# Own buffers for single-head ropes, an earlier zero for the sigmoids, early weight units around the norms, and two banks for the sparse transposes in a two-layer hybrid trunk

## The chip, the cores and the metric

The kernel runs on one core of a Trainium2 chip. The metric is the device time of one execution in microseconds. A core has five engines with queues of their own: TensorE (PE, matrix products, with its weight loads listed as PEld), VectorE (DVE), ScalarE (ACT), GpSimd (POOL) and SyncE (SP, which here issues nearly all DMA transfers). Each queue runs in the order in which it was written; semaphores tie the queues together. SBUF is the on-chip memory of 128 partitions, and PSUM the eight banks into which PE writes.

## The reference

Two layers over 256 tokens of width 1024. Each layer makes one wide projection of `x`, runs three token mixers on slices of it, merges them by sigmoid gates, projects, normalises, and follows with a squared-ReLU MLP, a gated per-layer embedding and a second norm. All is float32.

```python
for i in range(DEPTH):                        # 2
    h = x @ w_in[i]                           # 1024 -> 6222 columns
    (fq, fk, fv, ff_logit, sq, sk, sv, dq, dk, dv, iq, ik, iw, g) = split_cols(h)
    o_fox = fox_attention(fq, fk, fv, log_sigmoid(ff_logit + b_forget[i]))   # 6 heads
    o_sb = stick_breaking_attention(sq, sk, sv)                              # 5 heads
    dq, dk, iq, ik = (rope(a, pos) for a in (dq, dk, iq, ik))
    o_dsa = dsa_attention(dq, dk, dv, iq, ik, iw)   # 5 heads, one key head, top 64 keys
    gates = sigmoid(g.reshape(b, s, 3, D_MODEL))
    merged = (gates[:, :, 0] * (o_fox @ w_up_fox[i]) + gates[:, :, 1] * (o_sb @ w_up_sb[i])
              + gates[:, :, 2] * (o_dsa @ w_up_dsa[i]))
    x = layer_norm(ALPHA * x + merged @ w_out[i], ln1_g[i], ln1_b[i])
    ffn = square(relu(x @ w_ff_in[i])) @ w_ff_out[i]        # width 4096
    ple = sigmoid(x @ w_ple_gate[i]) * (p[i] @ w_ple[i])
    x = layer_norm(ALPHA * x + ffn + ple, ln2_g[i], ln2_b[i])
```

## The kernel before

**Precision and weight units.** Each float32 operand is split into a high and a low part of the matmul type fp32r, and a product is three matmuls: high by high, high by low, low by high (`mm3`, L158). Weights are loaded in units of 512 KB or less, mostly 128 partitions by 2 blocks by 512 columns. `wunit` loads a unit into one of five `wr` buffers by SP (L99), ACT copies it to `wh` (L143) and DVE subtracts to get `wl` (L144); `wh` and `wl` have five buffers each. Every other float32 tile of 512 columns comes from the pool `t2k` with 22 buffers, tiles of 256 columns from `t1k`, 384 columns from `t15` with two buffers.

**Products.** `xstat` multiplies token blocks by a weight slice into two PSUM banks, one per tile of 128 tokens (`pg`, four banks); `wstat` does the transposed product into three. With `by_tile` the token tile 0 is finished first: high products unit by unit (`tile_high`, L211), then the low ones (`tile_low`, L216), then an optional step `mid`, then tile 1. The attention works in four other banks, `ps`.

**A layer in order.** The input projection runs product by product in the list `PRODUCTS`: values of fox, fox queries and keys, index queries (`iq1`, `iq2`), sparse queries and key (`dsa`, done by `c4_done`), stick-breaking (`sb`, a `wstat`), its values with the first sparse query (`sv`, done by `c3_done`), gates. Attention jobs from the list `JOBS` are interleaved with it, one step of each job in flight per 550 columns of product. After them come the gate sigmoids, the three up projections (`up_blocks`, L852 and L853 for the shared blocks), `gated` (products with the gates, L835), the output projection `w_out`, the first norm, the embedding gate product, the MLP in eight chunks (`ff_in`, `ff_out`), and the second norm with the next layer's embedding product and first gate product around it.

**Ropes.** `do_rope` multiplies a slice of PSUM by cosine and sine on DVE (L423, L425, L427) into two `t15` tiles, and POOL adds them (L430, or L432 where the result is doubled). `c2_done`, `c4_done` and `c3_done` use it for 1, 3, 4 and 1 heads. Two calls in a row share the two `t15` buffers.

**Sparse transposes.** `dsa_T` transposes the roped key into one `ps` bank (L636), four blocks of queries into a second (L641), the last query head into a third (L646), each followed by a split.

**Sigmoids.** Their bias tile `zero` is computed by DVE from `last[0]`, a column of the last attention head's transposed and split weights, which makes it wait for that split; the comparison always gives 0. This keeps ACT's table for sigmoids from being loaded amid exponentials.

**Norms.** `layer_norm` takes statistics on DVE, the power on POOL (L255) and two passes on DVE (L259, L261); then the tile is transposed by PE (L178) and split. In the output projection tile 0's norm runs while PE multiplies tile 1; tile 1's norm runs while PE does the embedding product and tile 0 of the gate product. `second_x1T` and `second_T` transpose tile 1 as the `mid` step. At the layer's end the last `ff_out` is done tile by tile for the same reason, and all its four weight units stay in use to its end.

**The planner.** Instructions are put into the engines' queues by a planner that goes by program order among those that its own model of times says are ready, so an instruction late in the program can stand earlier in its queue. `keep_in_program_order` pins single instructions.

Of the kernel before, what the change touches and what calls it, by code (L numbers as in the profile page):

```python
# [16 lines left out]
P = 128  # L17
DM = 1024
T = 256
# [33 lines left out]
def hybrid_trunk(ctx, tc, x, p, w_in, b_forget, w_up_fox, w_up_sb, w_up_dsa, w_out,  # L53
# [25 lines left out]

    def t15(dt=F32R):  # L80
        return act.tile([P, 384], dt, tag="t15", name=nm("t15"), bufs=T15)

    def t16k(dt=F32R):

# [114 lines left out]
    def tok(aT, kb, t):  # L199
        return tuple(a[:, kb, t * P:(t + 1) * P] for a in aT)  # L200

    def xstat(aT, w, l, c0, n, done, nkb=KB, nk=2, by_tile=False, mid=None):


        o = [pg(), pg()]
        units = []

        def tile_high(t, u, wt):
            for kk in range(nk):
                for i in range(2):  # L210
                    nc.tensor.matmul(o[t][:, :n], tok(aT, u * nk + kk, t)[0], wt[i][:, kk, :],  # L211
                                     start=u + kk + i == 0, stop=False)

        def tile_low(t):
            for kb in range(nkb):
                nc.tensor.matmul(o[t][:, :n], tok(aT, kb, t)[1], units[kb // nk][0][:, kb % nk, :],  # L216
                                 start=False, stop=kb == nkb - 1)
            done(t, o[t])

        for u in range(nkb // nk):  # L220
            wt = wunit(wrows(w, l, u * nk, nk, c0, n), nk, n)
            units.append(wt)
            if by_tile:
                tile_high(0, u, wt)
                if u == nkb // nk - 1:
                    tile_low(0)
                    if mid:
                        mid()
                    for v, wt in enumerate(units):
                        tile_high(1, v, wt)  # L230
                    tile_low(1)
            else:
                for t in range(2):
                    for kk in range(nk):
                        kb = u * nk + kk
                        mm3(o[t][:, :n], tok(aT, kb, t), tuple(v[:, kk, :] for v in wt),
                            kb == 0, kb == nkb - 1)
# [54 lines left out]
            nc.scalar.copy(pe[j, t], o)  # L292
        return f

    def ple_products(l, pn):

        q = ps()
        for t in range(2):
            for b in range(2):
                nc.tensor.transpose(q[:, b * T + t * P:b * T + (t + 1) * P], pn[:, t, b * P:(b + 1) * P], ident)  # L300
        pT = tuple(t2k().rearrange("p (k t) -> p k t", t=T) for _ in range(2))
        split(q.rearrange("p (k t) -> p k t", t=T), *pT)

        for j in range(2):
            run(xstat(pT, w_ple, l, j * 512, 512, ple_done(j), nkb=2, nk=2))
            yield

    pe = {}
# [101 lines left out]
    bf = cst.tile([P, L, H_FOX], F32, name="bf")  # L410

    for l in range(L):
        if l:
            tc.keep_in_program_order(nc.scalar.preload_act_table_set("natural_log_exp_and_others"))
        vhl = t16k()[:, 0:3584].rearrange("p (i t c) -> p i t c", i=2, t=2)
        vh, vl = vhl[:, 0], vhl[:, 1]

        def do_rope(t, src, nh, dst, dup=1):

            s3 = src.rearrange("p (h d) -> p h d", d=HD)  # L420
            a = t15(F32)[:, :nh * HD].rearrange("p (h d) -> p h d", d=HD)
            b = t15(F32)[:, :nh * HD].rearrange("p (h d) -> p h d", d=HD)
            nc.vector.tensor_mul(a, s3, rope[:, t, None, :].to_broadcast([P, nh, HD]))  # L423
            hf = HD // 2
            nc.vector.tensor_mul(b[:, :, 0:hf], s3[:, :, hf:HD],  # L425
                                 rope[:, 2 + t, None, 0:hf].to_broadcast([P, nh, hf]))
            nc.vector.tensor_mul(b[:, :, hf:HD], s3[:, :, 0:hf],  # L427
                                 rope[:, 2 + t, None, hf:HD].to_broadcast([P, nh, hf]))
            if dup == 1:
                nc.gpsimd.tensor_add(dst.rearrange("p (h d) -> p h d", d=HD), a, b)  # L430
            else:
                nc.gpsimd.tensor_add(dst.rearrange("p (h d) -> p h d", d=HD),  # L432
                                     a.to_broadcast([P, dup, HD]), b.to_broadcast([P, dup, HD]))
# [1 line left out]

        gates = {}

        def gate(c):
            def done(t, o):
                g = t2k(F32)  # L440
                nc.scalar.copy(g, o)
                gates[c, t] = g
            return xstat(xT, w_in, l, O_G + c * 512, 512, done, by_tile=c == 0,
                         mid=second_T if c == 0 else None)

        def second_T():
            for j in range(2):
                to_xT(1, j)

        if l:  # L450
            run(gate(0))
        else:
            for u in range(1, KB // 2):
                wt = wunit(wrows(w_in, 0, 2 * u, 2, O_G, 512), 2, 512)
                if u == 1:
                    for t, o in ple_o:
# [159 lines left out]

        def c4_done(t, o):
            split(o[:, 320:384], vh[:, t, 768:832], vl[:, t, 768:832])
            do_rope(t, o[:, 0:256], 4, rnd[t][:, 64:320])
            do_rope(t, o[:, 256:320], 1, rnk[t][:, 128:256], dup=2)  # L620
            nc.gpsimd.tensor_copy(rnd[t][:, 320:384], rnk[t][:, 128:192])
            for v in (vh, vl):
                nc.gpsimd.tensor_copy(v[:, t, 832:896], v[:, t, 768:832])
# [9 lines left out]
        def dsa_T():  # L633
            q = ps()
            for t in range(2):
                nc.tensor.transpose(q[:, t * P:(t + 1) * P], rnk[t][:, 128:256], ident)  # L636
            split(q[:, 0:256], *dkT)
            q = ps()
            for b in range(2):
                for t in range(2):  # L640
                    nc.tensor.transpose(q[:, b * T + t * P:b * T + (t + 1) * P],  # L641
                                        rnd[t][:, b * P:(b + 1) * P], ident)
            split(q, *dqT, scale=-SCALE)
            q = ps()
            for t in range(2):
                nc.tensor.transpose(q[:, t * P:(t + 1) * P], rnd[t][:, 256:384], ident)  # L646
            split(q[:, 0:256], *dq4, scale=-SCALE)
            yield


# [24 lines left out]
        def softmax_heads(n, heads, mask):  # L675
# [12 lines left out]
            for i, s in enumerate(ss):  # L688
                mn = small(8)
                for t, sl in tiles:  # L690
                    nc.vector.tensor_tensor_reduce(pr[:, i, sl], s[:, sl], mask(t), 1.0, 3e38,
                                                   ALU.add, ALU.min, mn[:, t:t + 1])
                for t, sl in tiles:
                    nc.scalar.activation(pr[:, i, sl], pr[:, i, sl], AF.Exp, bias=mn[:, t:t + 1],
                                         scale=-1.0, accum_out=mn[:, 2 + t:3 + t])
                nc.vector.reciprocal(mn[:, 4:6], mn[:, 2:4])
                for t, sl in tiles:
                    nc.vector.tensor_scalar(pr[:, i, sl], pr[:, i, sl], mn[:, 4 + t:5 + t], None,
                                            op0=ALU.mult)
                yield  # L700
            pT = (t3k(), t3k())
            for i in range(len(heads)):
# [1 line left out]

                transpose_to(q, [pr[:, i, c * P:(c + 1) * P] for c in range(3)])
                split(q[:, 0:384], pT[0][:, i, :], pT[1][:, i, :])
                last[0] = pT[1].bitcast(F32)[:, i, 0:1]
                yield
            values(n, len(heads), pT)
            yield  # L710
# [274 lines left out]
        next(step)  # L985
        merged(1)
        run(step)
        run(xstat(mT, w_out, l, 512, 512, out_done(1), by_tile=True))


        def pgate_done(j):
# [9 lines left out]
            for j in range(2):  # L1001
                to_x1T(1, j)

        run(xstat(x1T, w_ple_gate, l, 0, 512, pgate_done(0), by_tile=True, mid=second_x1T))


        acc = [[pg() for _ in range(2)] for _ in range(2)]
# [43 lines left out]
        prev = None  # L1051
        for c in range(NC):
            hs = ff_in(c)
            if prev is not None:
                ff_out(c - 1, prev)
            else:
# [1 line left out]
            prev = hs  # L1058
        lg2, lb2 = ln_params(ln2_g, ln2_b, l)
        if l < L - 1:  # L1060
            p1 = load_p(l + 1)
        ff_out(NC - 1, prev)


# [3 lines left out]
        for t in range(2):  # L1068
# [7 lines left out]
            if l < L - 1:  # L1076
                layer_norm(t, st, lg2, lb2, None)
                if t == 0:
                    ple = ple_products(l + 1, p1)
                    next(ple)  # L1080
                    for j in range(2):
                        to_xT(0, j)
# [38 lines left out]
```

## Time and profile before

| | |
|---|---|
| median of 3 runs | 873.22 us (873.03 to 873.7) |
| profiled execution | 872.19 us, span 870.5 us |
| PE busy | 852.0 us (98%) |
| DVE busy | 642.2 us (74%) |
| ACT busy | 472.2 us (54%) |
| POOL busy | 70.2 us (8%) |
| read from HBM | 152.30 MB, mean 177 GB/s moved |
| granted PE clock | 0.997 |

The span is the time from the first to the last instruction of the profiled execution; the device time lies 1.7 us over it. A row of the timeline gives start, duration, engine, line, operation, the tiles written and read, shapes, and in brackets the idle time of that engine before it with what ended it. A row of the waits gives who waited for whom, the total in us, the times and the longest. PE's durations overlap, since matmuls are pipelined: a 128x512 product takes 0.39 us from start to end, and the next begins 0.23 us after it.

### The profile page before, as it was taken

How to read it: one execution, taken by the hardware profiler on the slowest of the kernel's cores; microseconds unless marked ns; L12 is line 12 of the kernel's file. 1: busy time of each engine (PE TensorE's matmuls, PEld its weight loads, DVE VectorE, ACT ScalarE, POOL GpSimd, SP SyncE). 2: the span in 40 equal slices, each digit the busy share in tenths (PEclk: the TensorE clock that was granted, in tenths of full speed). 3: DMA queues.
4: the chain of work that ended last, by engine and by line, in shares of the span. 5: the costliest groups of instructions: out<-in, count | busy, mean ns of one | idle time of the engine just before them, and what ended most of it. 6: DMA issues, size and time to landing. Idle time of an engine off the chain costs nothing.

```text
span 870.5 us, 12949 instructions
## 1 busy us (share of the span) xinstructions
PE 852.0 (98%) x4687; PEld 731.7 (84%) x4687; DVE 642.2 (74%) x1135; ACT 472.2 (54%) x749; POOL 70.2 (8%) x136
## 2 busy tenths in 40 slices
PE   8999999999999999999999999999999999999996
PEld 6998978878788888888879988888787888888885
DVE  6579997779867666666776899868887776666666
ACT  5456667676355444444454566677834654444440
POOL 1013010100011000000000221001001010000100
PEclk9999999999999999999999999999999999999998
DMA  8654665534566666666446647556274656666741
GB/s 286 197 148 125 204 190 166 173 126 161 184 217 199 187 193 192 191 217 217 129 137 176 163 129 221 162 165 184 76 248 136 227 191 190 193 192 194 235 128 49
DMA packets 80209, 154.46 MB, mean 177 GB/s; under 512 B 10257, under 2 KB 25745, under 8 KB 80145
## 3 DMA queue, kind: packets, MB, share of 16 engines
q1 hardware_dynamic: 78544, 149.17, 55.7%
q0 software_dynamic: 1600, 4.46, 1.7%
q8 instruction: 37, 0.61, 0.3%
q14 instruction: 28, 0.22, 0.1%
HBM read 152.30 MB, written 1.05 MB: 176 GB/s over the span
## 4 chain that ended last, share of the span: by engine, by line
PE 45%; DVE 3%; issue 1%; ACT 1%; DMA 0%; POOL 0%; POOLq 0%; DVEq 0%
PE pg L158 24%; PE ps L1017 7%; PE ps L1021 4%; PE pg L211 2%; PE pg L216 1%; PE pg L480 1%; PE pg L483 1%; PE pg L482 1%; DVE wl L144 1%; PE ps L165 1%; PE ps L178 1%; PE ps L158 1%; DMA wr<-in_w_in_dram 0%; DVE x L261 0%; ACT wh L143 0%
## 5 line engine op out<-in xcount | busy, mean ns | idle before, releaser
L144 DVE TENSOR_TENSOR wl<-wr,wh 128x1024 fp32r<-128x1024 f32 (+4 forms) x300 | 340.9, 1148 | 169.0 <-ACT wh L143 167.8
L143 ACT CAST wh<-wr 128x1024 fp32r<-128x1024 f32 (+4 forms) x300 | 292.9, 986 | 292.9 <-PE pg L158 109.2
L158 PE MATMUL pg<-wh,t16k 128*128 128x512 f32 (+4 forms) x792 | 231.1, 366 | 0.1
L158 PE MATMUL pg<-wh,t2k 128*128 128x512 f32 x536 | 168.1, 390 | 0.2 <-ACT t2k L143 0.2
L158 PEld LDWEIGHTS pg<-wh,t16k 128*128 128x128 f32 x792 | 144.4, 188 | 20.7 <-DVE t2k L151 0.7
L158 PE MATMUL pg<-wl,t16k 128*128 128x512 f32 (+4 forms) x396 | 143.6, 363 | 0.3 <-DVE wl L144 0.3
L1017 PE MATMUL ps<-t16k,wh 128*128 128x512 f32 x512 | 127.8, 391 | 0.0
L158 PEld LDWEIGHTS pg<-wh,t2k 128*128 128x128 f32 x536 | 100.7, 188 | 21.1 <-ACT t2k L143 0.4
L1017 PEld LDWEIGHTS ps<-t16k,wh 128*128 128x128 f32 x512 | 93.1, 189 | 17.3
L158 PE MATMUL pg<-wl,t2k 128*128 128x512 f32 x268 | 104.4, 390 | 0.0
L158 PEld LDWEIGHTS pg<-wl,t16k 128*128 128x128 f32 x396 | 74.4, 188 | 9.1 <-DVE wl L144 0.7
L1021 PEld LDWEIGHTS ps<-t16k,wl 128*128 128x128 f32 x512 | 69.8, 190 | 5.0
L1021 PE MATMUL ps<-t16k,wl 128*128 128x256 f32 x512 | 71.4, 282 | 0.0
L158 PEld LDWEIGHTS pg<-wl,t2k 128*128 128x128 f32 x268 | 50.4, 188 | 9.9
L480 PE MATMUL pg<-t16k,wh 128*128 128x256 f32 x176 | 50.5, 287 | 2.9 <-DVE t L427 2.9
L483 PE MATMUL pg<-t16k,wl 128*128 128x256 f32 x176 | 49.8, 283 | 0.0
L482 PE MATMUL pg<-t16k,wh 128*128 128x256 f32 x176 | 49.7, 283 | 0.0
L158 PE MATMUL pg<-wh,t1k 128*128 128x512 f32 x112 | 37.9, 396 | 0.0
L480 PEld LDWEIGHTS pg<-t16k,wh 128*128 128x128 f32 x176 | 33.6, 191 | 3.4 <-issue 3.3
L482 PEld LDWEIGHTS pg<-t16k,wh 128*128 128x128 f32 x176 | 33.7, 191 | 0.0
L483 PEld LDWEIGHTS pg<-t16k,wl 128*128 128x128 f32 x176 | 33.7, 191 | 0.0
L211 PE MATMUL pg<-wh,t16k 128*128 128x512 f32 x80 | 31.5, 394 | 0.6 <-ACT t16k L143 0.6
(196 smaller groups left out, 969.8 us busy)
## 6 DMA issues: line engine op xcount, KB each, us to landing
wr<-in_w_ff_in_dram SPq DMA_DIRECT2D x64, 512.0 KB, 4.4
wr<-in_w_ff_out_dram SPq DMA_DIRECT2D x64, 512.0 KB, 4.1
wr<-in_w_in_dram SPq DMA_DIRECT2D x47, 512.0 KB, 4.2
wr<-in_w_in_dram SPq DMA_DIRECT2D x32, 384.0 KB, 3.7
wr<-in_w_out_dram SPq DMA_DIRECT2D x16, 512.0 KB, 4.4
wr<-in_w_ple_gate_dram SPq DMA_DIRECT2D x16, 512.0 KB, 5.0
wr<-in_w_in_dram SPq DMA_DIRECT2D x16, 256.0 KB, 2.9
wr<-in_w_in_dram SPq DMA_DIRECT2D x8, 390.0 KB, 3.3
```

What stands on the lines that cost most here:

```text
L143: a = nc.scalar.copy(hi, src)
L144: b = nc.vector.tensor_sub(lo, src, hi.bitcast(F32))
L158: nc.tensor.matmul(o, l, r, start=start and i == 0, stop=stop and i == 2, skip_group_check=skip)
L165: nc.tensor.matmul(o, a[i == 2], b[i == 1], start=start and i == 0, stop=stop and i == 2)
L178: tr = nc.tensor.transpose(dst[:, i * P:(i + 1) * P], s, ident)
L211: nc.tensor.matmul(o[t][:, :n], tok(aT, u * nk + kk, t)[0], wt[i][:, kk, :], start=u + kk + i == 0, stop=False)
L216: nc.tensor.matmul(o[t][:, :n], tok(aT, kb, t)[1], units[kb // nk][0][:, kb % nk, :], start=False, stop=kb == nkb - 1)
L480: nc.tensor.matmul(oi, hi, rh, start=kb == 0 and i % 2 == 0, stop=False, skip_group_check=True)
L482: nc.tensor.matmul(oi, hi, rl, start=False, stop=False, skip_group_check=True)
L483: nc.tensor.matmul(oi, lo, rh, start=False, stop=kb == KB - 1, skip_group_check=True)
L1017: nc.tensor.matmul(pz[i], wt[0][:, kk, i * P:(i + 1) * P], x1_both[:, 2 * u + kk, :], start=u + kk == 0, stop=False, skip_group_check=True)
L1021: nc.tensor.matmul(pz[i][:, 0:T], wt[1][:, kk, i * P:(i + 1) * P], x1T[0][:, 2 * u + kk, :], start=False, stop=2 * u + kk == KB - 1, skip_ ...
```

## The change

It has five edits.

- `rope_parts`: a rope of one head takes one tile of a new two-buffer tag `t05` instead of two `t15` tiles. In `c4_done` the key's rope stands before the four-head rope.
- `dsa_T`: the last query head's transposes go into the second half of the key's bank; the reads are two on ACT, then two on DVE.
- `last[0]` is set to the softmax reciprocal instead of a column of the split weights.
- `early_unit` loads a weight unit and splits it block by block into four `t2k` tiles instead of `wh` and `wl`. `xstat` takes such units through `early`. One is made for the embedding gate before the last step of the output projection; one each for the next layer's embedding product and first gate in the last MLP chunk, where `p` is now loaded too. `p_T` transposes `p` before the last `ff_out`. `mid` moves from behind `tile_low(0)` into its middle.
- The load of the table for exponentials moves from the start of layer 2 to the third MLP chunk of layer 1.

```diff
+    def rope_parts(nh):
+        if nh == 1:
+            ab = act.tile([P, 2 * HD], F32, tag="t05", name=nm("t05"), bufs=2)
+            return [ab[:, i * HD:(i + 1) * HD].rearrange("p (h d) -> p h d", d=HD) for i in range(2)]
+        return [t15(F32)[:, :nh * HD].rearrange("p (h d) -> p h d", d=HD) for _ in range(2)]
...
+    def early_unit(srcs, nk, n):
+        raw = wload(srcs, nk, n)
+        hi, lo = [t2k() for _ in range(nk)], [t2k() for _ in range(nk)]
+        for kk in range(nk):
+            split(raw[:, kk, :], hi[kk], lo[kk])
+        return hi, lo
...
-        def tile_low(t):
+        def tile_low(t, mid=None):
             for kb in range(nkb):
+                if mid and kb == nkb // 2:
+                    mid()
...
         for u in range(nkb // nk):
-            wt = wunit(wrows(w, l, u * nk, nk, c0, n), nk, n)
+            wt = early[u] if u < len(early) else blocks_of(
+                wunit(wrows(w, l, u * nk, nk, c0, n), nk, n), nk)
...
                 if u == nkb // nk - 1:
-                    tile_low(0)
-                    if mid:
-                        mid()
+                    tile_low(0, mid)
...
     for l in range(L):
-        if l:
-            tc.keep_in_program_order(nc.scalar.preload_act_table_set("natural_log_exp_and_others"))
...
         if l:
-            run(gate(0))
+            run(gate(0, gate_early))
...
             split(o[:, 320:384], vh[:, t, 768:832], vl[:, t, 768:832])
+            do_rope(t, o[:, 256:320], 1, rnk[t][:, 128:256], dup=2)
             do_rope(t, o[:, 0:256], 4, rnd[t][:, 64:320])
-            do_rope(t, o[:, 256:320], 1, rnk[t][:, 128:256], dup=2)
...
-            split(q[:, 0:256], *dkT)
+            for t in range(2):
+                nc.tensor.transpose(q[:, T + t * P:T + (t + 1) * P], rnd[t][:, 256:384], ident)
+            k, q4 = q[:, 0:T], q[:, T:2 * T]
+            nc.scalar.copy(dkT[0], k)
+            nc.scalar.activation(dq4[0], q4, AF.Copy, scale=-SCALE)
+            nc.vector.tensor_sub(dkT[1], k, dkT[0].bitcast(F32))
+            nc.vector.scalar_tensor_tensor(dq4[1], q4, -SCALE, dq4[0].bitcast(F32), op0=ALU.mult,
+                                           op1=ALU.subtract)
...
-            q = ps()
-            for t in range(2):
-                nc.tensor.transpose(q[:, t * P:(t + 1) * P], rnd[t][:, 256:384], ident)
-            split(q[:, 0:256], *dq4, scale=-SCALE)
...
                 nc.vector.reciprocal(mn[:, 4:6], mn[:, 2:4])
+                last[0] = mn[:, 4:5]
...
-                last[0] = pT[1].bitcast(F32)[:, i, 0:1]
...
-        run(xstat(mT, w_out, l, 512, 512, out_done(1), by_tile=True))
+        step = xstat(mT, w_out, l, 512, 512, out_done(1), by_tile=True)
+        for _ in range(3):
+            next(step)
+        pgate_early = [early_unit(wrows(w_ple_gate, l, 0, 2, 0, 512), 2, 512)]
+        run(step)
...
             hs = ff_in(c)
+            if c == 2 and l < L - 1:
+                tc.keep_in_program_order(nc.scalar.preload_act_table_set("natural_log_exp_and_others"))
+            if c == NC - 1 and l < L - 1:
+                p1 = load_p(l + 1)
+                ple_early = [early_unit(wrows(w_ple, l + 1, 0, 2, 0, 512), 2, 512)]
+                gate_early = [early_unit(wrows(w_in, l + 1, 0, 2, O_G, 512), 2, 512)]
...
         if l < L - 1:
-            p1 = load_p(l + 1)
+            pT1 = p_T(p1)
         ff_out(NC - 1, prev)
```

More of the change, by code (lines that the diff above doesn't have):

```diff
@@ L200, in tok, with blocks_of, xstat @@
         return tuple(a[:, kb, t * P:(t + 1) * P] for a in aT)
-    def xstat(aT, w, l, c0, n, done, nkb=KB, nk=2, by_tile=False, mid=None):
+    def early_unit(srcs, nk, n):
[4 more added lines that the diff above has]
+        return hi, lo
+    def blocks_of(wt, nk):
+        return tuple([v[:, kk, :] for kk in range(nk)] for v in wt)
+    def xstat(aT, w, l, c0, n, done, nkb=KB, nk=2, by_tile=False, mid=None, early=()):
         o = [pg(), pg()]
@@ L210, in tile_high @@
                 for i in range(2):
-                    nc.tensor.matmul(o[t][:, :n], tok(aT, u * nk + kk, t)[0], wt[i][:, kk, :],
+                    nc.tensor.matmul(o[t][:, :n], tok(aT, u * nk + kk, t)[0], wt[i][kk],
                                      start=u + kk + i == 0, stop=False)
-        def tile_low(t):
+        def tile_low(t, mid=None):
             for kb in range(nkb):
-                nc.tensor.matmul(o[t][:, :n], tok(aT, kb, t)[1], units[kb // nk][0][:, kb % nk, :],
+                if mid and kb == nkb // 2:
+                    mid()
+                nc.tensor.matmul(o[t][:, :n], tok(aT, kb, t)[1], units[kb // nk][0][kb % nk],
                                  start=False, stop=kb == nkb - 1)
@@ L235, in xstat @@
                         kb = u * nk + kk
-                        mm3(o[t][:, :n], tok(aT, kb, t), tuple(v[:, kk, :] for v in wt),
+                        mm3(o[t][:, :n], tok(aT, kb, t), tuple(v[kk] for v in wt),
                             kb == 0, kb == nkb - 1)
@@ L293, in ple_done, with p_T @@
         return f
-    def ple_products(l, pn):
+    def p_T(pn):
         q = ps()
@@ L302, in ple_products @@
         split(q.rearrange("p (k t) -> p k t", t=T), *pT)
+        return pT
+    def ple_products(l, pT, early=()):
         for j in range(2):
-            run(xstat(pT, w_ple, l, j * 512, 512, ple_done(j), nkb=2, nk=2))
+            run(xstat(pT, w_ple, l, j * 512, 512, ple_done(j), nkb=2, early=early if j == 0 else ()))
             yield
@@ L420, in do_rope @@
             s3 = src.rearrange("p (h d) -> p h d", d=HD)
-            a = t15(F32)[:, :nh * HD].rearrange("p (h d) -> p h d", d=HD)
-            b = t15(F32)[:, :nh * HD].rearrange("p (h d) -> p h d", d=HD)
+            a, b = rope_parts(nh)
             nc.vector.tensor_mul(a, s3, rope[:, t, None, :].to_broadcast([P, nh, HD]))
@@ L436, in hybrid_trunk, with gate @@
         gates = {}
-        def gate(c):
+        def gate(c, early=()):
             def done(t, o):
@@ L443, in gate @@
             return xstat(xT, w_in, l, O_G + c * 512, 512, done, by_tile=c == 0,
-                         mid=second_T if c == 0 else None)
+                         mid=second_T if c == 0 else None, early=early)
         def second_T():
@@ L1002, in second_x1T @@
                 to_x1T(1, j)
-        run(xstat(x1T, w_ple_gate, l, 0, 512, pgate_done(0), by_tile=True, mid=second_x1T))
+        run(xstat(x1T, w_ple_gate, l, 0, 512, pgate_done(0), by_tile=True, mid=second_x1T,
+                  early=pgate_early))
         acc = [[pg() for _ in range(2)] for _ in range(2)]
@@ L1078, in hybrid_trunk @@
                 if t == 0:
-                    ple = ple_products(l + 1, p1)
+                    ple = ple_products(l + 1, pT1, ple_early)
                     next(ple)
```

## The prediction

> **What bounds the kernel now.** I read the engine totals first, then the busy time by stage, then who TensorE (PE) waited for, and last the timeline around each wait.
>
> ```profile
> PE 852.0 (98%) x4687; PEld 731.7 (84%) x4687; DVE 642.2 (74%) x1135; ACT 472.2 (54%) x749; POOL 70.2 (8%) x136
> ```
> ```profile
> core 0: us, PE busy (x) PEld busy (x) DVE busy (x) ACT busy (x) POOL busy (x), PEclk, DMA share, GB/s
> 70.00:113.00 43.00, 41.55 (x316) 38.74 (x315) 40.78 (x116) 26.47 (x54) 9.77 (x20) 1.00 0.60 173
> 113.00:180.00 67.00, 66.67 (x345) 54.60 (x344) 53.43 (x118) 45.65 (x86) 6.52 (x14) 1.00 0.58 174
> 180.00:200.00 20.00, 18.95 (x90) 15.34 (x89) 15.58 (x27) 17.34 (x27) 0.00 (x0) 1.00 0.24 79
> 228.00:245.00 17.00, 16.67 (x79) 13.21 (x79) 13.45 (x19) 8.59 (x13) 2.41 (x2) 1.00 0.50 155
> 433.00:452.00 19.00, 17.79 (x85) 13.61 (x84) 13.64 (x21) 10.10 (x15) 0.99 (x1) 1.00 0.37 105
> 500.00:543.00 43.00, 41.17 (x313) 37.93 (x312) 40.50 (x115) 26.57 (x52) 8.46 (x19) 1.00 0.59 170
> 610.00:630.00 20.00, 18.94 (x92) 15.40 (x91) 15.92 (x25) 17.34 (x27) 0.00 (x0) 1.00 0.23 80
> 657.00:675.00 18.00, 17.68 (x83) 14.06 (x84) 13.46 (x20) 9.74 (x14) 2.39 (x2) 1.00 0.47 146
> 857.00:870.50 13.50, 5.33 (x24) 4.09 (x22) 10.34 (x20) 0.00 (x0) 1.98 (x2) 0.80 0.21 78
> ```
> ```profile
> PE pg L480 <- DVE t L427: 2.9, 2, 1.5
> PE pg L852 <- DVE t2k L835: 2.1, 2, 1.1
> PE ps L178 <- DVE x L261: 0.9, 1, 0.9
> PE ps L646 <- DVE t1k L144: 0.7, 2, 0.3
> ```
>
> PE is the bound: 852.0 of 870.5 us. The change adds no matmul and removes none, so it can only give back idle time of PE. The last stage (8.2 us idle) is the end of the last norm, which the change leaves alone. The eight stages above it hold 1.45 + 0.33 + 1.05 + 0.33 + 1.21 + 1.83 + 1.06 + 0.32 = 7.6 us of idle. That is nearly all there is to win, a little more where a matmul starts late without a gap. The waits name four of the places, each once per layer except L178, which is the change of layer.
>
> **Part A, ropes.** The single-head rope gets buffers of its own, and in `c4_done` the one-head key rope now stands ahead of the four-head query rope.
>
> ```profile
> 78.84 0.73 POOL L430 TENSOR_TENSOR t2k<-t,t 128x256 f32<-128x256 f32 x1 [0.25 <-DVE t L427]
> 78.95 1.30 DVE L144 TENSOR_TENSOR wl<-wr,wh 128x640 fp32r<-128x640 f32 x1
> 80.40 0.18 DVE L427 TENSOR_TENSOR t<-pg,rope 128x32 f32<-128x32 f32 x1
> 80.73 0.36 PE L480 MATMUL pg<-t16k,wh 128*128 128x256 f32 x1 [1.42 <-DVE t L427]
> ```
>
> PE waits at 80.73 for a PSUM bank that the key rope of tile 0 still reads. The key rope could not start before POOL had added the query rope (both `t15` buffers taken), so a weight split of 1.30 us went ahead of it on DVE. With own buffers the key rope is three short instructions (0.1 to 0.2 us each) ahead of the query rope, which ends just before the add at 78.84. The bank is then free near 79.3, where PE's gap begins (80.73 less 1.42): 1.42 us goes, 1.46 us in layer 2 by the same wait (2.9 in the list). But DVE is busy 40.78 of 43 us here, and what it did in PE's gap it must do later. The nearest bound for the gain is from 0 (DVE carries it all on) to 2.9. I take 2.4, near the upper end, because the weight splits run far ahead of PE: counted in order, the one at 78.95 is for the fifth block of a product of which PE is at the first at 80.73. What is late next is the work behind it in the same DVE queue, the top-k and the ropes of the next product.
>
> The two POOL rows that follow bear on what DVE's and POOL's overlap costs.
>
> ```profile
> 109.97 0.32 POOL L430 TENSOR_TENSOR t2k<-t,t 128x64 f32<-128x64 f32 x1
> 110.66 1.22 DVE L144 TENSOR_TENSOR wl<-wr,wh 128x1024 fp32r<-128x1024 f32 x1
> 110.82 1.24 POOL L430 TENSOR_TENSOR t2k<-t,t 128x64 f32<-128x64 f32 x1 [0.24 <-DVE t L427]
> 112.27 0.60 PE L641 MATMUL ps<-ident,t2k 128*128 128x128 f32 x4
> ```
>
> The same add takes 0.32 us alone and 1.24 beside a split, and it ends at 112.06, just ahead of the transposes that need it. So if PE comes here 1.4 us early and DVE does not, up to 1.2 us per layer of part A returns as a wait. [...]
>
> **Part B, sparse transposes.** The last pair of transposes moves into the bank of the first pair.
>
> ```profile
> 113.42 0.42 DVE L144 TENSOR_TENSOR t1k<-ps,t1k 128x256 fp32r<-128x256 f32 x1
> 113.90 0.44 PE L646 MATMUL ps<-ident,t2k 128*128 128x128 f32 x2 [0.33 <-DVE t1k L144]
> ```
>
> PE waited for the first of three banks to be read out; with two banks this wait is gone, 0.33 us each (0.7 in the list). Transposes and reads keep their number and size. Bounds: gain 0.7; or 0, if the second bank waits instead, since ACT now reads two tensors out of the first. I take 0.6.
>
> **Part C, the sigmoids' zero.** The bias that holds the sigmoids back is made from the last softmax reciprocal instead of the last split of the transposed weights.
>
> ```profile
> 179.53 0.17 DVE L696 RECIPROCAL small<-small 128x2 f32<-128x2 f32 x1 [0.74 <-ACT t3k L694]
> 184.79 1.06 ACT L143 CAST wh<-wr 128x1024 fp32r<-128x1024 f32 x1 [1.60 <-issue]
> 187.35 0.54 DVE L144 TENSOR_TENSOR t3k<-ps,t3k 128x384 fp32r<-128x384 f32 x1
> 187.85 1.28 ACT L961 ACT_TABLE_LOAD   x1
> 190.65 0.50 PE L852 MATMUL pg<-wh,t1k 128*128 128x512 f32 x1 [1.05 <-DVE t2k L835]
> 191.92 5.63 ACT L961 ACTIVATE t2k<-t2k,small 128x512 f32<-128x512 f32 x9
> ```
>
> The zero may now come at 179.7 instead of 187.9. All exponentials are over by then, so the table load (1.28 us) and the first sigmoids (0.63 us each, 5.63 over 9) fit in the ACT pauses before 187.85, such as the 1.60 us before 184.79. The gate products then free the banks before PE asks: 1.05 us per layer goes. Bounds: gain 2.1; loss under the first rival. I take 1.9.
>
> **Part D, the norm inside a layer.** One gate-weight unit is split during the output projection into `t2k` tiles, and the transposes of tile 1 move to the middle of tile 0's low products.
>
> ```profile
> 210.23 1.50 SPq L99 DMA_DIRECT2D wr<-in_w_out_dram  x2
> 213.10 0.37 SPq L99 DMA_DIRECT2D wr<-in_w_ple_dram  x1
> 217.00 1.05 ACT L143 CAST wh<-wr 128x1024 fp32r<-128x1024 f32 x1 [1.94 <-DMA wr<-in_w_out_dram]
> 221.43 0.39 PE L211 MATMUL pg<-wl,t16k 128*128 128x512 f32 x1
> 224.13 0.69 DVE L975 SCALAR_TENSOR_TENSOR x<-x,pg 128x512 f32<-128x512 f32 x1 [1.88 <-PE pg L216]
> 240.44 0.50 PE L211 MATMUL pg<-wh,t16k 128*128 128x512 f32 x1 [0.29 <-ACT t16k L143]
> ```
>
> Behind the transposes PE waits for ACT's copy; four low products (0.23 us a start) now cover it. That is the 0.33 and 0.32 us of these stages; DVE is also rid of 1.22 us of split between the norm's steps. The price is on SP's queue: the early load stands ahead of the last unit of the output projection, which ACT already waits for at 217.00. The two issues from 210.23 are the last of that projection; one buffer later is 213.10, some 1.8 us after the second. Cast (1.05 from 217.00) and split (1.22) end near 219.3, 2.1 us before PE's use at 221.43, so nothing is lost. The early subtractions fit in DVE's 1.88 us pause before 224.13. If the load slips further, up to 1 us per layer is lost. Bounds +2.0 and -0.65; I take 0.6.
>
> **Part E, the change of layer.** One unit each of the embedding product and of the first gate, the transposes of `p`, and the table load move from here into the MLP.
>
> ```profile
> 431.53 2.95 ACT L143 CAST wh<-wr 128x1024 fp32r<-128x1024 f32 x3 [7.79 <-PE pg L158]
> 442.44 0.64 PE ps L178 x4
> ```
>
> At 431.53 ACT had waited 7.79 us for a `wh` buffer: the last MLP chunk holds four of the five, the embedding unit the fifth. With that unit and the first gate unit in `t2k`, the second gate unit gets the buffer, so two splits (1.22 each) and the smaller split of `p` leave DVE's way to tile 1's norm, over 2.4 us, against the 0.9 us for which PE waits at 442.44 (L178 in the list). The stage's idle is 1.21, and late starts stand beside it: I take 1.4; bounds 0 and 2. The three extra splits in halves and two loads fall in the MLP, where DVE is busy 16.15 of 22 us (the row below) and the DMA share is 0.50; without that cover each split would cost its 1.2 us. On SP the two loads and that of `p` go ahead of the last eight MLP units; no quoted row shows how late those may be. The `t2k` pool of 22 holds the eleven early tiles (four for each unit, three for `p`) only while nothing else of the chunk is late.
>
> ```profile
> 411.00:433.00 22.00, 22.00 (x101) 18.32 (x101) 16.15 (x24) 8.74 (x13) 1.00 (x1) 1.00 0.50 150
> ```
>
> **Sum.** 2.4 + 0.6 + 1.9 + 0.6 + 1.4 = 6.9 us. The profiled execution took 872.19 us (span 870.5), 1.0 under the median of 873.22; so 865.3 for such an execution and 866.3 for the median.
>
> **The rivals.** First, slower: ACT's order. Once the zero is early, all twelve sigmoids and the table load (9 us) may be put ahead of the casts that the last attention heads and the next weight units wait for. ACT has only 2.7 us of pauses in 180 to 200, so up to 6 us per layer would be late; some 2 us of it is covered by the prefetched units, and 4 us per layer, 8 in all, would turn the 5.0 us of the other parts into a loss of 3: 876. It decides from about 2.5 us per layer. For it: ACT is busy 17.34 of 20 us, and the nine sigmoids ran in one row. Against: the heads' casts come first in the program. [...]
>
> Second, DVE as the bound: in 70 to 113 and 500 to 543 it is 95% busy, and what A and B take out returns as waits behind its splits. Then 1.9 + 0.6 + 1.4 remain, less about 0.7: 870. Against: the splits' lead.
>
> Third, no change: orders shift all over the queues with the planner's times and new waits of a few tenths eat the gain: 873. Fourth, more than forecast: all idle goes and the late starts with it, 7.6 and some 2.1 us (an estimate: about twenty matmuls behind a wait take 0.50, as at 240.44, where the form takes 0.39, as at 221.43): 863.5.
>
> **How the numbers follow.** A difference of 0.2% (1.7 us) is about what a measurement of this kernel can tell from no change. Forecast 0.52, fourth rival 0.10, second 0.18 (all faster): 0.80. No change 0.09, slower 0.11. The forecast's own range is 864 to 869; to hold 8 in 10 it reaches from 863 to 871.5, over the fourth and second, and leaves out the other two (0.20).
>
> **What would show it.** A: no wait of L480 for a rope, the key rope ahead of the query rope. B: no wait at the second bank. C: the table load near 181 and no wait at L852; wrong, if the embedding or up units' casts come after the sigmoids and PE waits for `wl` near 193. D: PE straight from transposes into low products. E: no table load in this stage, tile 1's norm some 2 us sooner, idle in that stage under 0.4 us. The prediction is wrong if the stage from 70 to 113 keeps its 1.4 us of idle under other names.

## The result and the profile after

The changed kernel takes 867.8 us (mean of five executions, 866.8 to 869.6; their median is 867.3) against 873.3 us (mean of six, 872.7 to 873.8; median 873.4) for the kernel before, measured together: a ratio of 0.9937, 95% interval 0.9923 to 0.995, or 5.5 us less. The forecast was 866.3 us, with a range from 863.0 to 871.5. A sixth execution, the profiled one, ran at a granted clock of 0.56 and is left out of these figures, so the trace shown here is that of a repeat of the same kernel (`e1_after` below: median 867.97 us, profiled execution 867.06 us, span 865.3 us).

First the engine totals, then the busy time in the nine stages that the prediction showed (the windows are shifted so that they hold nearly the same work), then the rows of PE's waits that matter here.

```profile
PE 851.3 (98%) x4687; PEld 734.3 (85%) x4687; DVE 640.8 (74%) x1139; ACT 471.8 (55%) x753; POOL 65.8 (8%) x136
```
```profile
core 0: us, PE busy (x) PEld busy (x) DVE busy (x) ACT busy (x) POOL busy (x), PEclk, DMA share, GB/s
70.00:111.80 41.80, 41.58 (x310) 38.95 (x310) 39.45 (x118) 25.69 (x53) 8.06 (x21) 1.00 0.57 169
111.80:178.50 66.70, 66.70 (x358) 55.04 (x357) 54.00 (x116) 45.31 (x83) 7.10 (x15) 1.00 0.60 179
178.50:198.50 20.00, 18.97 (x91) 15.35 (x89) 14.32 (x26) 18.85 (x32) 0.00 (x0) 1.00 0.19 59
226.00:243.00 17.00, 16.96 (x83) 13.78 (x82) 15.72 (x26) 8.55 (x12) 3.29 (x3) 1.00 0.50 163
430.50:449.00 18.50, 18.21 (x89) 15.02 (x88) 13.76 (x21) 7.81 (x12) 1.32 (x2) 1.00 0.31 87
497.20:539.50 42.30, 42.08 (x318) 39.01 (x317) 39.69 (x112) 26.58 (x52) 7.33 (x18) 1.00 0.62 185
605.50:625.50 20.00, 18.82 (x90) 15.22 (x89) 15.44 (x24) 17.31 (x27) 0.00 (x0) 1.00 0.22 67
652.00:670.00 18.00, 17.96 (x87) 14.55 (x87) 15.27 (x22) 9.55 (x14) 3.19 (x3) 1.00 0.37 117
852.00:865.30 13.30, 5.18 (x23) 3.94 (x22) 10.18 (x20) 0.00 (x0) 1.98 (x2) 0.83 0.22 79
```
```profile
PE ps L165 <- ACT t3k L150: 1.6, 2, 0.8
PE pg L165 <- DVE wl L151: 1.1, 3, 0.4
PE pg L500 <- DVE t16k L151: 0.4, 2, 0.2
PE pg L230 <- ACT t16k L150: 0.3, 1, 0.3
```

Read the second fence by window length less PE busy. The rope stages fall from 1.45 and 1.83 us of idle to 0.22 each, the sparse stage after the first from 0.33 to 0.00, the norms inside the layers from 0.33 and 0.32 to 0.04 each, and the change of layer from 1.21 to 0.29. The two stages of the sigmoids do not fall: 1.05 and 1.06 before, 1.03 and 1.18 after. The eight stages together go from 7.6 to 3.0 us of idle.

Idle time is not the whole account: a matmul that starts late without a gap is not in it, and the spans of two traces also differ at the start. PE's 101st matmul is this one (first row before, second row after):

```profile
25.00 0.51 PE L158 MATMUL pg<-wh,t16k 128*128 128x390 f32 x2
26.67 0.51 PE L165 MATMUL pg<-wh,t16k 128*128 128x390 f32 x2
```

Up to it the instructions of every engine and the DMA issues stand in the same order in both kernels, and still the changed kernel is 1.67 us later. In the thirteen traces of this study (the kernel before and the twelve runs below), all with that order, this matmul starts between 25.00 and 27.52 us. So the stages are better compared by how much earlier the same-numbered matmul starts, from one stage to the next; PE has 4687 matmuls in every kernel, and where two kernels do not differ, this count stays within about 0.1 us. Counted so, the change gains 3.7 us in the rope stages and the sparse transposes behind them, loses 0.6 in the sigmoid stages, and gains 1.7 in the norms inside the layers and 2.0 up to and at the change of layer. That is 6.8 us behind the start; less the 1.7 us at the start it gives the 5.2 us by which the span fell.

The list of waits says why the sigmoid stages do not gain. The wait of the up projections for the gate products is gone (2.1 us in the list before). Two others have come: L165 for ACT's copy of attention weights (`t3k`), 1.6 us, and L165 for a weight split (`wl`), 1.1 us where it was 0.3. The timeline shows both:

```profile
180.04 0.15 DVE L981 TENSOR_SCALAR small<-small 128x1 f32<-128x1 f32 x1
181.16 1.28 ACT L984 ACT_TABLE_LOAD   x1
183.81 3.18 ACT L984 ACTIVATE t2k<-t2k,small 128x512 f32<-128x512 f32 x5
187.14 0.48 ACT L150 CAST t3k<-ps 128x384 fp32r<-128x384 f32 x1
187.68 0.49 PE L165 MATMUL ps<-t3k,t16k 128*128 128x512 f32 x1 [0.83 <-ACT t3k L150]
192.68 4.82 ACT L150 CAST wh<-wr 128x1024 fp32r<-128x1024 f32 x5
198.68 0.50 PE L165 MATMUL pg<-wl,t1k 128*128 128x512 f32 x1 [0.38 <-DVE wl L151]
```

The zero is early (180.04) and the table is loaded at 181.16, as forecast. But five sigmoids in a row go ahead of the last head's cast at 187.14, and PE waits 0.83 us for that cast. The weight casts come after all the sigmoids, five in a row from 192.68, and a split is late: DVE makes it from 197.41 on, behind four gate products, and PE has waited 0.38 us when it starts at 198.68. This second wait is gone in `e6_two` and `e9_early_table` below, where ten or all of the sigmoids take the late zero. The transposes that the cast at 187.14 reads were done at 185.92 (three from 185.43, 0.49 us), and the cast ran only after the sigmoids. It is the first rival's mechanism, at 1.2 us per layer in the list.

### The profile page after: what moved, and what is told of

Same layout as the page of the kernel before. It is cut to its first block, busy times and chain, and to the rows that moved or that the text cites. A ratio compares the mean times of both kernels' runs of the same rounds, so it can differ in the third digit from the quotient of the medians.

```text
span 1411.4 us, 12935 instructions
## 1 busy us (share of the span) xinstructions
PE 1401.1 (99%) x4687; PEld 945.7 (67%) x4687; DVE 651.0 (46%) x1139; ACT 476.8 (34%) x753; POOL 61.9 (4%) x136
## 3 DMA queue, kind: packets, MB, share of 16 engines
HBM read 152.30 MB, written 1.05 MB: 109 GB/s over the span
## 4 chain that ended last, share of the span: by engine, by line
PE 98%; issue 1%; DVE 0%; POOL 0%; POOLq 0%
PE pg L165 54%; PE ps L1045 14%; PE ps L1049 7%; PE pg L230 4%; PE pg L500 2%; PE pg L503 2%; PE pg L502 2%; PE ps L172 2%; PE ps L185 2%; PE pg L237 2%; PE ps L165 2%; PE pg L351 1%; PE pg L876 0%; PE pg L875 0%; PE ps L821 0%
## 5 line engine op out<-in xcount | busy, mean ns | idle before, releaser
L165 PE MATMUL pg<-wh,t16k 128*128 128x512 f32 (+4 forms) x792 | 347.8, 527 | 0.0
L165 PE MATMUL pg<-wh,t2k 128*128 128x512 f32 x528 | 257.4, 577 | 0.0
L165 PEld LDWEIGHTS pg<-wh,t16k 128*128 128x128 f32 x792 | 175.7, 225 | 87.5 <-issue 40.9
L1045 PE MATMUL ps<-t16k,wh 128*128 128x512 f32 x512 | 208.8, 575 | 0.0
L165 PE MATMUL pg<-wl,t16k 128*128 128x512 f32 (+4 forms) x396 | 208.6, 527 | 0.0
L165 PEld LDWEIGHTS pg<-wh,t2k 128*128 128x128 f32 x528 | 116.0, 220 | 84.2 <-issue 48.3
L165 PE MATMUL pg<-wl,t2k 128*128 128x512 f32 x264 | 152.0, 576 | 0.0
L1049 PEld LDWEIGHTS ps<-t16k,wl 128*128 128x128 f32 x512 | 103.3, 237 | 22.7 <-issue 12.7
L165 PEld LDWEIGHTS pg<-wl,t16k 128*128 128x128 f32 x396 | 90.6, 229 | 41.6 <-issue 20.3
L1049 PE MATMUL ps<-t16k,wl 128*128 128x256 f32 x512 | 110.6, 385 | 0.0
L165 PEld LDWEIGHTS pg<-wl,t2k 128*128 128x128 f32 x264 | 58.1, 220 | 41.2 <-issue 23.3
L500 PE MATMUL pg<-t16k,wh 128*128 128x256 f32 x176 | 68.5, 389 | 0.0
L502 PE MATMUL pg<-t16k,wh 128*128 128x256 f32 x176 | 67.0, 381 | 0.0
L165 PE MATMUL pg<-wh,t1k 128*128 128x512 f32 x112 | 57.0, 584 | 0.0
L502 PEld LDWEIGHTS pg<-t16k,wh 128*128 128x128 f32 x176 | 50.0, 284 | 0.5 <-issue 0.2
L500 PEld LDWEIGHTS pg<-t16k,wh 128*128 128x128 f32 x176 | 49.4, 281 | 0.8
L230 PE MATMUL pg<-wl,t16k 128*128 128x512 f32 x68 | 38.9, 577 | 0.0
```

Source lines behind the costliest of these rows:

```text
L165: nc.tensor.matmul(o, l, r, start=start and i == 0, stop=stop and i == 2, skip_group_check=skip)
L500: nc.tensor.matmul(oi, hi, rh, start=kb == 0 and i % 2 == 0, stop=False, skip_group_check=True)
L502: nc.tensor.matmul(oi, hi, rl, start=False, stop=False, skip_group_check=True)
L1045: nc.tensor.matmul(pz[i], wt[0][:, kk, i * P:(i + 1) * P], x1_both[:, 2 * u + kk, :], start=u + kk == 0, stop=False, skip_group_check=True)
L1049: nc.tensor.matmul(pz[i][:, 0:T], wt[1][:, kk, i * P:(i + 1) * P], x1T[0][:, 2 * u + kk, :], start=False, stop=2 * u + kk == KB - 1, skip_ ...
```

## The experiments

Letters are those of the prediction: A ropes, B banks, C zero, D norm inside a layer, E change of layer. Each run was timed against the kernel before on the same chip; the median of before was 873.5 beside e1 to e4, 873.6 beside e5 to e8 and 873.7 beside e9 to e12. A gain or loss in us is the ratio's distance from 1 times 873.5. "Counted by matmul" means the comparison of starts described above, which leaves out the start of the kernel. Line numbers differ from kernel to kernel; the tiles name the places.

**e1_after.** The whole change once more. 

> The whole change again, for a trace at the full clock. Forecast's theory (PE's idle comes back where the waits were): 5 to 7 us faster than before, PE idle in 70 to 113 and 500 to 543 under 0.5 us each, in 180 to 200 and 610 to 630 under 0.3, in the change of layer under 0.4. Rival (DVE is the bound beside the ropes): the same total, but the 1.4 us beside the ropes are still idle under another name, and the gain comes from the sigmoids and norms alone.

Measured: 867.97 us, ratio 0.9937 (0.9925 to 0.9949). By the stages above, the expectation held for the ropes and the change of layer and failed for the sigmoids.

**e2_ropes.** Part A alone.

```diff
+        if nh == 1:
+            ab = act.tile([P, 2 * HD], F32, tag="t05", name=nm("t05"), bufs=2)
...
+            do_rope(t, o[:, 256:320], 1, rnk[t][:, 128:256], dup=2)
             do_rope(t, o[:, 0:256], 4, rnd[t][:, 64:320])
-            do_rope(t, o[:, 256:320], 1, rnk[t][:, 128:256], dup=2)
```

> The kernel before with part A alone (own buffers and key rope first). Forecast's theory: 2.4 us faster (0.9973), L480 waits for no rope. Rival, DVE as the bound: under 0.8 us faster, the gap moves to later waits on DVE or POOL in the same 40 us.

Measured: 871.31 us, ratio 0.9971 (0.9959 to 0.9982), 2.5 us less; counted by matmul, 1.2 and 1.3 us in the two rope stages. In its list of waits the 2.9 us for the rope have become 0.4 us for a split of values at the same matmul:

```profile
PE pg L514 <- DVE t16k L161: 0.4, 2, 0.2
```

**e3_zero.** Part C alone.

```diff
+                last[0] = mn[:, 4:5]
...
-                last[0] = pT[1].bitcast(F32)[:, i, 0:1]
```

> The kernel before with part C alone (zero from the last reciprocal). Forecast's theory: 1.9 us faster (0.9978), the table load stands near 181. Rival, sigmoids in front of the casts: no gain or slower, PE waits for wl of the up units near 193.

Measured: 874.39 us, ratio 1.001 (1.0001 to 1.0019): 0.9 us slower (0.1 to 1.7), where 1.9 us less was forecast. Counted by matmul, the two sigmoid stages lose 0.5 us. Its waits show the same exchange as in the whole change, the gate products' 2.1 us gone and these two come or grown:

```profile
PE ps L175 <- ACT t3k L160: 1.6, 2, 0.8
PE pg L175 <- DVE wl L161: 1.0, 3, 0.4
```

**e4_norms.** Parts D and E alone: the early units, the earlier `p`, its early transposes, the table load, and the transposes of tile 1 at mid product.

```diff
-                    tile_low(0)
-                    if mid:
-                        mid()
+                    tile_low(0, mid)
...
+        pgate_early = [early_unit(wrows(w_ple_gate, l, 0, 2, 0, 512), 2, 512)]
...
+                p1 = load_p(l + 1)
+                ple_early = [early_unit(wrows(w_ple, l + 1, 0, 2, 0, 512), 2, 512)]
+                gate_early = [early_unit(wrows(w_in, l + 1, 0, 2, O_G, 512), 2, 512)]
```

> The kernel before with parts D and E (early units, transposes of p earlier, table load in the MLP, tile 1's transposes amid the low products). Forecast's theory: 0.6 + 1.4 = 2.0 us faster (0.9977). Rival, the early load delays the output projection's last unit: D loses up to 1 us per layer and the sum is 0.6 us slower to 0.6 us faster.

Measured: 873.06 us, ratio 0.9999 (0.999 to 1.0008), level. Nothing is left of a forecast of 2.0 us. The timeline of the norm inside the first layer has a wait that neither the kernel before nor the whole change has:

```profile
230.99 2.35 DVE L161 TENSOR_TENSOR wl<-wr,wh 128x1024 fp32r<-128x1024 f32 x2
235.06 1.22 DVE L161 TENSOR_TENSOR wl<-wr,wh 128x1024 fp32r<-128x1024 f32 x1
236.80 1.21 DVE L161 TENSOR_TENSOR wl<-wr,wh 128x1024 fp32r<-128x1024 f32 x1
238.04 1.17 DVE L161 TENSOR_TENSOR wl<-wr,wh 128x1024 fp32r<-128x1024 f32 x1
240.52 1.41 DVE L293 SCALAR_TENSOR_TENSOR x<-x,small,t2k 128x512 f32<-128x512 f32 x2
241.41 1.29 PE L195 MATMUL ps<-ident,x 128*128 128x128 f32 x8 [0.90 <-DVE x L293]
```

DVE makes five weight splits (the first row counts two) between tile 0's and tile 1's norm; the last (238.04) ends just before the two passes of tile 1's norm, and PE waits 0.90 us for them. In the whole change there are three in that stretch:

```profile
230.66 1.22 DVE L151 TENSOR_TENSOR wl<-wr,wh 128x1024 fp32r<-128x1024 f32 x1
233.60 1.21 DVE L151 TENSOR_TENSOR wl<-wr,wh 128x1024 fp32r<-128x1024 f32 x1
234.84 1.17 DVE L151 TENSOR_TENSOR wl<-wr,wh 128x1024 fp32r<-128x1024 f32 x1
238.52 0.60 PE L185 MATMUL ps<-ident,x 128*128 128x128 f32 x4
238.64 1.22 DVE L151 TENSOR_TENSOR wl<-wr,wh 128x1024 fp32r<-128x1024 f32 x1
```

Which splits they are follows from counting, and is the same in both layers. The kernel before has four here, one for each unit of the embedding gate. The early unit leaves three of these, so two of the five in `e4_norms` belong to the first MLP units; in the whole change the MLP's first (238.64) stands behind the norm.

**e5_nozero.** The whole change without part C. 

> The whole change without part C (zero from the last split, as before). If the parts simply add, as measured alone, C costs 0.9 us and this is 6.5 us faster than before. Theory now: C also sets where the planner puts the split of the first MLP weight unit; without C that split stands ahead of tile 1's norm, PE waits about 1.2 us per layer for x at the gate product, and this is only 3.5 to 4 us faster than before, slower than the whole change by about 1.8 us.

Measured: 869.83 us, ratio 0.9959 (0.9947 to 0.9971). Both the old wait for the gate products and the new one for the norm are there:

```profile
PE pg L911 <- DVE t2k L894: 2.1, 2, 1.1
PE ps L195 <- DVE x L293: 1.8, 2, 0.9
```

So part C, which loses 0.9 us alone, gains 1.9 us beside the others (0.9959 less 0.9937), since with it the planner puts those MLP splits behind the norm. In the two lists: 2.1 + 1.8 us of waits go, 1.6 + 0.8 come. Counted by matmul, C gains 3.1 us in the two norm stages and loses 0.6 in the sigmoid stages.

**e6_two.** The whole change, but only the first two of each layer's twelve sigmoids take the early zero.

```diff
-                nc.scalar.activation(gates[c, t], gates[c, t], AF.Sigmoid, bias=zero)
+                nc.scalar.activation(gates[c, t], gates[c, t], AF.Sigmoid,
+                                     bias=zeros["early" if c in (0,) else "late"])
```

> The whole change, but only the first two of the twelve sigmoids take the early zero, the other ten the late one. Theory (the early sigmoids hold up the last head's casts on ACT): PE's 0.8 us wait per layer for the last head's split goes and its wait for the first gate product stays away, so 1.5 to 2.5 us faster than the whole change, 7 to 8 us faster than before. Rival (the late weight casts are what costs): no faster than the whole change.

Measured: 869.16 us, ratio 0.9946 (0.9934 to 0.9958). The expectation failed: this is not faster than the whole change. Two sigmoids are enough to make PE wait, for the same cast and for another:

```profile
PE ps L175 <- ACT t3k L160: 1.0, 2, 0.5
PE pg L175 <- ACT t1k L160: 0.8, 2, 0.4
PE pg L363 <- ACT wh L160: 1.6, 1, 1.6
```

The third row is at the kernel's start, where the whole change waits 0.9 us at the same matmul; that 0.7 us is not the sigmoids'. Counted by matmul, the sigmoid stages are no better than in the whole change.

**e7_norms_pinned.** As `e4_norms`, with the cast and split of the first MLP unit held in program order, behind the norm.

```diff
+                pinned[0] = c == 0 and u == 0
                 wt = wunit(wrows(w_ff_in, l, 2 * u, 2, c * 512, 512), 2, 512)
+                pinned[0] = 0
```

> Parts D and E alone as in the fourth run, with one thing more: the split of the first MLP weight unit is pinned in program order, behind the norm of tile 1. Theory (a place freed on DVE was taken by that split): PE's wait of 0.9 us per layer before the transposes in the gate product goes, and this is 2.5 to 3.5 us faster than before, where the fourth run was level. Rival (PE only comes too early because the transposes stand sooner): the wait stays and the time is level.

Measured: 875.3 us, ratio 1.0019 (1.001 to 1.0029), slower than `e4_norms`. The wait for the norm is gone, as expected; the held cast now makes PE wait in the MLP, and `p` comes late:

```profile
PE ps L1083 <- ACT wh L160: 3.2, 2, 1.6
PE ps L332 <- DMA pn<-in_p_dram: 2.0, 1, 2.0
```

So the five splits are what delays the norm, but pinning is no cure.

**e8_banks.** Part B alone: `dsa_T` as in the diff above. 

> Part B alone (two banks for the sparse transposes). Theory: the two waits of the third bank go, 0.7 to 1.0 us faster than before. Rival (the second bank waits instead): level, with PE waiting at the second bank's transposes.

Measured: 872.52 us, ratio 0.9989 (0.998 to 0.9997), 1.0 us less. The wait of 0.7 us is not in its list, and none at the second bank.

**e9_early_table.** All twelve sigmoids keep the late zero; one sigmoid of a single column takes the early one, so that ACT's table comes early alone.

```diff
+        nc.vector.tensor_scalar(pre, first[0], -2.0, None, op0=ALU.is_lt)
+        nc.scalar.activation(pre, pre, AF.Sigmoid)
         nc.vector.tensor_scalar(zero, last[0], -2.0, None, op0=ALU.is_lt)
```

> The whole change, except that the twelve sigmoids keep the late zero of the kernel before; only one sigmoid of a single column per layer takes the early zero, so that ACT's table load still comes early. Theory: the table load is what made PE wait for the gate products (1.2 us per layer), and the sigmoids queued ahead of casts are what made the two new waits (1.55 us per layer). Then all three go, about 3 us less than the whole change, but the weight split of the MLP ahead of tile 1's norm comes back with its 1.06 us per layer: 866 to 867.5 us, table load near 181 us, no wait for ACT t3k of the last heads. Rival: the wait for the gate products comes from the nine sigmoids themselves; it stays, and the time is that of the whole change without part C, 869.8.

Measured: 869.3 us, ratio 0.995 (0.9937 to 0.9964), nearer to the rival's 869.8. Both theories hold in part: the waits for `t3k` and for the second `wl` are gone and the norm's is back, but of the wait for the gate products half is left.

```profile
PE ps L195 <- DVE x L293: 1.8, 2, 0.9
PE pg L909 <- DVE t2k L892: 1.0, 2, 0.5
```

Why half, a row of the kernel before tells. There the late zero itself is made here, later than the 187.9 that the prediction gave it:

```profile
188.38 0.15 DVE L958 TENSOR_SCALAR small<-t3k 128x1 f32<-128x1 f32 x1
```

It is done at 188.53, but the table load ends only at 189.13 (1.28 us from 187.85), and the first sigmoid follows. So the table was 0.6 us later than the zero, and an early table can win no more of the 1.05 us. Counted by matmul, it gains 0.6 us per layer over `e5_nozero`.

**e10_table_no_unit.** As e9, without the early unit of the embedding gate (`pgate_early` is an empty list). 

> As e9_early_table, but without the early unit of the embedding gate, so that this product loads its first unit as in the kernel before. Theory: the early unit's free weight buffer is what pulls an MLP split ahead of tile 1's norm; without it DVE has four splits there instead of five and the 1.06 us per layer goes, at the price of at most 0.45 us per layer that the kernel before lost behind its transposes: 864.5 to 865.8 us, the fastest so far. Rival: the extra split is harmless and the early unit saves what part D said (0.3 us per layer): 867 to 868, slower than e9_early_table.

Measured: 866.42 us (864.9 to 867.2), ratio 0.9912 (0.9899 to 0.9926): 3.3 us under e9, and the lowest time of the study, though its interval still touches that of the whole change. The wait for the norm is gone from its list. `p` landed late in the profiled execution:

```profile
414.95 0.47 SPq L110 DMA_DIRECT2D pn<-in_p_dram  x1
422.42 0.63 PE L332 MATMUL ps<-ident,pn 128*128 128x128 f32 x4 [2.12 <-DMA pn<-in_p_dram]
```

**e11_table_split_late.** As e9 with its early unit, but DVE's subtraction of the first MLP unit held behind the norm, with ACT's cast left free. 

> As e9_early_table with its early unit, but DVE's subtraction of the first MLP unit is held in program order, behind tile 1's norm; ACT's cast of it is left free. DVE then has two splits fewer ahead of that norm. Theory: the 1.06 us per layer goes and nothing takes its place, since PE needs these splits only some 8 us later: 864.5 to 865.5. Rival: the splits put off come too late for the MLP and PE waits for them there, as it did in e7_norms_pinned: 866.5 or more.

Measured: 869.6 us, ratio 0.9946 (0.9933 to 0.996). The rival was right. The wait for the norm goes and others come in the MLP:

```profile
PE pg L176 <- ACT wh L160: 1.6, 2, 0.8
PE ps L1088 <- DVE wl L161: 1.2, 2, 0.6
```

**e12_layer_change.** Part E with the transposes at mid product, without the early unit of the embedding gate. 

> Part E alone with the transposes at mid product: the early units for the next layer's embedding product and gate, the early transposes of p and the earlier table load, but not the early unit of the embedding gate. The prediction's value of E is 1.4 and of the moved transposes some 0.6: 871.2 to 872.2 if it holds. D and E together measured 0.0 to 0.5, so the early unit of the embedding gate would then cost 1.3 to 2 us by itself (theory: 1.06 us per layer). Rival: E gains nothing and D costs nothing: 873.1.

Measured: 870.66 us, ratio 0.9964 (0.9951 to 0.9976), 3.1 us less. `e4_norms` has one thing more, the early unit of the embedding gate, and gains 0.1. That unit therefore costs 3.0 us in this company, and 3.3 us between e9 and e10. Counted by matmul it is 2.4 and 2.5 us, all in the two norm stages. Four splits instead of five stand ahead of the norm, and the stage of the norm and the change of layer hold as little idle (0.04 and 0.29 us) as in the whole change:

```profile
226.00:245.00 19.00, 18.96 (x90) 15.06 (x89) 16.96 (x26) 8.55 (x12) 3.29 (x3) 1.00 0.47 149
433.00:451.00 18.00, 17.71 (x86) 14.62 (x85) 13.40 (x21) 7.67 (x12) 0.99 (x1) 1.00 0.31 89
```

## Why the prediction was right, and where it was not

The median came out 1.0 us above the forecast, well inside its range. Term by term:

**A, 2.4 forecast, 2.5 measured alone.** The mechanism and the size hold: the wait went and DVE did not carry its work on to the next wait. The limit that was feared beside it, POOL's add against a split, did come, in both layers alike (1.24 us at 111.16, 1.23 at 535.57), as before the change (1.24 at 110.82, 1.23 at 539.67); here it is in the first:

```profile
111.00 1.21 DVE L151 TENSOR_TENSOR wl<-wr,wh 128x1024 fp32r<-128x1024 f32 x1
111.16 1.24 POOL L450 TENSOR_TENSOR t2k<-t 128x64 f32<-128x64 f32 x1
111.51 0.97 PE L172 MATMUL ps<-t1k,t2k 64*128 64x256 f32 x12
112.41 0.44 PE L656 MATMUL ps<-ident,t1k 128*128 128x128 f32 x2
```

Here the add takes 1.24 us beside the split; the same add of the tile before, at 110.44, ahead of that split, took 0.32. It cost no wait that the list shows: PE had twelve matmuls of another job to run (111.51 to 112.4) until it was done. An add 0.92 us longer on POOL was no wait of PE here.

**B, 0.6 forecast, 1.0 measured** (0.3 to 1.7 by the interval). The wait went as told; the size agrees within the interval.

**C, 1.9 forecast, and alone 0.9 us slower.** This is the step that failed: "the table load (1.28 us) and the first sigmoids ... fit in the ACT pauses before 187.85". The table load did fit; the sigmoids did not stop at the pauses. All that are ready stand in ACT's queue ahead of casts that become ready a little later, and PE waits for those (0.83 us at 187.68). "The heads' casts come first in the program" was the argument against this rival, and it does not hold: program order is only the planner's second criterion, as the text on the planner says. The sign of being wrong that the prediction named for this part came too: casts after the sigmoids and a wait for `wl`, at 198.68. The rival's place was right, but its price, given as 4 us per layer, was 1.2 in the list (1.6 + 0.8 over both layers). It took back the whole gain and, counted by matmul, 0.6 us more. e9 then shows what the early table is worth by itself. The wait for the gate products falls from 2.1 to 1.0 us without sigmoids in front of the casts; what is left comes of the late zero.

**D, 0.6 forecast; the early unit loses 3.0 to 3.3 us where C is absent or reduced to the table.** The working priced the early load on SP's queue, which was harmless (no wait of PE for a load of the output projection stands in the lists of `e1_after` and `e4_norms`), and credited DVE with 1.22 us less before the norm. It did not ask what the planner would do with the weight buffers that the early unit leaves free. DVE got other splits instead, those of the MLP, in the same place. In the whole change part C happens to put them behind the norm, so D's stage loses its idle there as forecast, and gains 1.7 us counted by matmul. The moved transposes do that without the early unit too (e12, 0.04 us of idle).

**E, 1.4 forecast; with the moved transposes 3.1 measured** (2.1 to 4.3), against the 2.0 forecast for D and E together. The place was right: stage idle 0.29 us for "under 0.4", and those 0.3 us are PE's wait at L230 for ACT's copy of the transposed tile. Counted by matmul, `e12_layer_change` gains 1.7 us up to and at the change of layer (E) and 1.0 in the norms inside the layers (the moved transposes). A size somewhat above the forecast fits the late starts that the term's upper bound of 2 took in.

**The sum.** The parts alone give 2.5 + 1.0 - 0.9 + 0.1 = 2.7 us, and the whole gives 5.5. The difference is the meeting of C and D: C's new waits (2.4 us) are paid in either case, but only with C are the MLP splits out of the norm's way. C's presence moved the time by the 1.9 us forecast for it (e5 against e1), for a reason that the prediction did not have. Counted by matmul in the whole change, A and B bring 3.7 us (3.0 forecast), C loses 0.6 (a gain of 1.9 forecast), D brings 1.7 (0.6) and E 2.0 (1.4). That these 6.8 us lie so near the forecast's 6.9 is luck: what C fell short by, 2.5 us, the others brought above their terms. The times gave 5.5; whether the later start of the changed kernel's trace stands behind the difference was not settled.

Nor was it settled why the planner, with the early unit in place, puts no MLP split ahead of the norm with twelve early sigmoids, one with two (e6) and two with one or none, in both layers alike; the runs show the orders and their prices, not its reckoning. The early unit was not taken out of the whole change with C as it stands.

## What to carry to other kernels

Where queues are filled by a planner, a change of one part is priced together with the orders that it brings about elsewhere. Take the parts singly and all but one at a time: here one part was a loss alone and a gain in company, and an early unit that the forecast credited was a loss in both kernels from which it was taken out. A bias or flag that holds back work on one engine can protect other work of that engine: here the sigmoids let go early made PE wait 2.4 us in the list for casts and a split; releasing only the table load kept half of the gain (the wait for the gate products fell from 2.1 to 1.0 us), and without the early unit it gave the lowest time, 866.4 us. Compare two traces stage by stage and from behind the start, since the start alone differed by up to 2.5 us here.

## What was not expected of the hardware

The load of `p`, 256 KB, has no fixed latency in this place. In e10 PE's transposes waited until 422.42 for it, some 7.5 us after its issue at 414.95. In the whole change they ran 5.2 us after the issue and without a wait:

```profile
416.59 0.47 SPq L100 DMA_DIRECT2D pn<-in_p_dram  x1
421.79 0.60 PE L320 MATMUL ps<-ident,pn 128*128 128x128 f32 x4
```

From issue to landing it took 4.4 us in the whole change and 7.3 us in e10; over the nine kernels that load it early, 4.4 to 7.3 us. The weight loads beside it were the same in both: one unit issued 0.4 us before it and the next 2.7 us after it. In e10 these took longer too (5.2 and 5.9 us against 4.2 and 4.5). An early load that is just early enough in one kernel's execution cost 2 us in another's, and these runs do not show why.
